# A transformer block on one core: instruction order from another timing model, pair sums split once, and two late loads in a chain of their own

## The chip, the cores and the metric

The kernel runs on one core of a Trainium2 chip. The metric is the device time of one execution in microseconds (us). The core has five engines that take instructions from queues of their own, each in order: TensorE (PE, with its weight loads listed apart as PEld), VectorE (DVE), ScalarE (ACT), GpSimd (POOL) and SyncE (SP), whose queue issues nearly all loads here.

## The reference, cut to what matters

One block over 512 tokens of width 1024, in float32. Eight heads use dilated attention ("a" heads), eight use compressed, selected and window attention with gates ("b" heads). A vector `c` gives shifts, scales and gate rows.

```python
mod = silu(c) @ w_ada + b_ada
sh1, sc1, g1, sh2, sc2, g2 = split(mod, 6)
u = layer_norm(x) * (1 + sc1) + sh1
o_a = dilated_attention(rope(qa), rope(ka), va)
o_b = nsa_attention(rope(qb), kc, vc, ks, vs, kw, vw, gates, ...)
y = concat([o_a, o_b]) @ w_o
x = layer_norm(ALPHA * x + g1 * y, ln1_g, ln1_b)
u = layer_norm(x) * (1 + sc2) + sh2
a_gate, a_val = split(u @ w_up, 2)
h = gelu(causal_dwconv(a_gate, conv_w, conv_b)) * a_val
x = layer_norm(ALPHA * x + g2 * (h @ w_down), ln2_g, ln2_b)
```

## The kernel before, in words

Every matrix operand is a pair: a value rounded to the matmul type (`hi`) and the rest (`lo`). `split` (L255) makes the two: ACT copies to `hi`, DVE or POOL subtracts. `mm3` (L259) then makes three matmuls, hi·hi, hi·lo, lo·hi (lines L260 to L262).

The stages are these. From 0 to about 66 us: layer norm of `x`, its transposes, the scale and shift columns of `c` (L351, on DVE), and the first product. From 66 to about 334 us: the attention rows, with the other input products ("quads", L1141 to L1148) as filler between them. From 334 to 380 us: the product with `w_o`, the residual norm and the second `u`. From 380 to 734 us: the up product (22 column blocks) and the down product (22 row blocks). At the end: the last norm and the output.

**The attention loop** (L1304 to L1320) has an iteration counter k over 76 rows and 5 more iterations. In each iteration the letters of `SEQ` say what is emitted: scores, weights, exponent, transposes and use of rows at fixed distances, filler matmuls (`f`), and four times `m`, which advances one background chain by one step (`run_misc`, L1084). A chain is a generator; `yield n` means that its next step comes no sooner than n calls of `run_misc` later. A row is emitted for scores at iteration k and its weighted sum ("use") five iterations later.

**The late chain.** `AUX = ['kvg3']` (L117) makes one chain (`late_steps`, L1057), started before the loop: first the compressed keys (`k`: four weight loads, then matmuls L1163), then the compressed values (`v`, the same), then the gate row g1 (`g`: `ada_row`, L1036, with eight loads of 512 KB and eight DVE sums, L1020 and L1022, a bias row L1043 and two pairs of matmuls L1048), then the shift vector of the second norm (`3`: eight loads `ada_col`, eight DVE reductions L1031). All these loads, those of the quads (`w_quad`, L1117) and of `w_o` use the four buffers `wraw` (`NR = 4`), and all are issued in order by SP.

**Sums of the heads.** The weighted sum of a head pair lies in one PSUM bank (`pv`, one buffer), in two halves of 64 partitions for e = 0 and e = 1. `folded` (L791) copies one half with ACT (L796) into a `wk` buffer (three of them) and hands it on. For a dilated pair `fold_a` (L827) does the following for e = 0 and again for e = 1, each time on 64 partitions: DVE adds (L829), DVE rounds to `oh` (L834), POOL subtracts to `ol` (L838). For a "b" pair `fold_b` (L800) adds into `ysum`, `cmp_end` (L886) adds the compressed part, and `pair_split` (L846) rounds with DVE (L848) and subtracts with POOL (L852), on 128 partitions.

**Order.** Within `tile.TileContext` the framework does not keep the order in which the code is written: it keeps dependences, and orders each engine's instructions by a simulated execution in which an instruction is dispatched when its inputs are ready. On the chip this order is fixed: an instruction whose input is late holds up all behind it on its engine.

Of the kernel before, what the change touches and what calls it, by code (L numbers as in the profile page):

```python
# [11 lines left out]
F32R = mybir.dt.float32r  # L12
PSUM = bass.MemoryType.PSUM
ALU = mybir.AluOpType
AF = mybir.ActivationFunctionType
# [91 lines left out]
def body(ctx, tc, nc, a, out, dbg=None):  # L107
    dbg = dbg or {}
    FILL = (2, 2, 3, 4)
    GAP = 4  # L110
# [3 lines left out]
    HG = 12  # L114
    WG = 4
    WK = 70
    AUX = ['kvg3']  # L117
    CP = 0
    YBS = (2, 3)
    OWK = ()  # L120
    FA = 1
# [21 lines left out]
    FS = 1  # L143
    QS = 1
# [23 lines left out]
    V, A, P, T = nc.vector, nc.scalar, nc.gpsimd, nc.tensor  # L168
# [4 lines left out]
    def slot(tag, bufs, shape, dt=F32, name=None):  # L173
        return sb.tile(shape, dt, name=name or tag, tag=tag, bufs=bufs)
# [7 lines left out]
    def to(name, dt=F32R):  # L182
        return slot('o', NO, [128, 512], dt, name)

    def u8(name):
        return slot('u2', 4, [128, 4, 512], F32R, name)
# [11 lines left out]
    def wraw(shape=(128, 1024)):  # L198
        return slot('wr', NR, list(shape), F32, 'wraw')
# [7 lines left out]
    def wk(name, dt=F32):  # L207
        return slot('wk', NW, [128, 512], dt, name)
# [7 lines left out]
    wlive = [0]  # L216

    def wk_wait(n):
        while wlive[0] + n > NW:
            yield 'wait'  # L220
        wlive[0] += n
# [15 lines left out]
    def f(x):  # L237
        return x.bitcast(F32)

    def load(dst, src, queue=nc.sync):  # L240
        queue.dma_start(dst, src)
# [13 lines left out]
    def split(raw, hi, lo, lo_engine=V):  # L255
        A.activation(hi, raw, AF.Copy)  # L256
        lo_engine.tensor_sub(lo, raw, f(hi))  # L257
# [61 lines left out]
    for t in range(NT):  # L319
# [7 lines left out]
        else:  # L327
            nb = offset_of(ag, P if NBP else V)
            cs = [slice(0, 1024)]
            if t == 3:  # L330
                cs = [slice(0, X3), slice(X3, 1024)]
                if XV:
                    c = cs.pop(0)
# [38 lines left out]
    for j in range(KD):  # L372
# [18 lines left out]
        for term in terms:  # L391
            for i in range(2):
                cs = slice(256 * i, 256 * i + 256)
                for t in range(NT):
                    tk = slice(128 * t, 128 * t + 128)
                    o_ = accs[i][t // 2][:, 256 * (t % 2):256 * (t % 2) + 256]
# [388 lines left out]
        return [row(tiles) for tiles in ((0, 1), (2,), (3,))]  # L785

    oh, ol = [None] * 8, [None] * 8
    ysum = [None] * 4
    done_o = set()

    def folded(pv, e):  # L791

        mn, ot = (0, 64) if e == 0 else (64, 0)
        yield from wk_wait(1)
        half = wk('fold')[mn:mn + 64]
        A.activation(half, pv[ot:ot + 64], AF.Copy)  # L796
        yield 2
        return half, pv[mn:mn + 64], slice(mn, mn + 64)
# [23 lines left out]
    def cmp_mm(h, pv, first):  # L822
        r = slice(64 * (h % 2), 64 * (h % 2) + 64)
        for i, (s_, p_) in enumerate(((0, 'h'), (1, 'h'), (0, 'l'))):
            T.matmul(pv, vpad[0][r, s_, :], pc[p_][h // 2][r], start=first and i == 0, stop=i == 2)

    def fold_a(idx, pv, e):  # L827
        half, own, mn = yield from folded(pv, e)
        V.tensor_add(half, own, half)  # L829
        if e == 0:  # L830
            mk = wk if idx in OWK else to
            oh[idx], ol[idx] = to('oh', F32R), mk('ol', F32R)
        yield 1
        (V.tensor_copy if FA else lambda o_, i_: A.activation(o_, i_, AF.Copy))(oh[idx][mn], half)  # L834
        yield 1
        for x in range(FS):
            c = slice(512 // FS * x, 512 // FS * (x + 1))
            P.tensor_sub(ol[idx][mn][:, c], half[:, c], f(oh[idx][mn][:, c]))  # L838
            if x < FS - 1:
                yield 1  # L840
        wlive[0] -= 1
        if e == 1:
            done_o.add(idx)
        yield 1

    def pair_split(h):  # L846
        oh[h], ol[h] = to('oh'), to('ol')
        V.tensor_copy(oh[h], ysum[h])  # L848
        yield 1
        for x in range(QS):  # L850
            c = slice(512 // QS * x, 512 // QS * (x + 1))
            P.tensor_sub(ol[h][:, c], ysum[h][:, c], f(oh[h][:, c]))  # L852
            if x < QS - 1:
                yield 1
        done_o.add(h)

    held = {}

# [166 lines left out]
    def ada_late_cols(gap, which=(2, 3)):  # L1025
        for i in which:
            for j in range(KD):
                w = wgem()
                load(w, a['ada_col'][j, i])
                yield gap  # L1030
                V.tensor_tensor_reduce(w, w, crow, 1.0, 0.0, op0=ALU.mult, op1=ALU.add, accum_out=mod[:, i, j:j + 1])  # L1031
            V.tensor_add(mod[:, i, :], mod[:, i, :], bcol[:, i, :])
            if i == 2:
                V.tensor_scalar_add(mod[:, 2, :], mod[:, 2, :], 1.0)

    def ada_row(s, out_, gap=None):  # L1036
        res = []
        yield from ada_sum(s, res, gap)
        acc = res[0]
        b1 = wgem()  # L1040
        load(b1[0:1, :], a['b_row'][s:s + 1, :])
        yield gap
        V.tensor_add(acc[0:1, :], acc[0:1, :], b1[0:1, :])  # L1043
        yield 2
        for h in range(2):
            yield from acc_wait()
            pr = acc_bank('gr')
            T.matmul(pr, ones, acc[:, 512 * h:512 * h + 512], start=True, stop=True)  # L1048
            yield 2
            A.activation(acc[:, 512 * h:512 * h + 512], pr, AF.Copy)  # L1050
            acc_done()
        out_.append(acc)
        yield

    g1l, g2l = [], []

    def late_steps(gap, AUX):  # L1057
        for c in AUX:
            if c == 'k':
                yield from hidden(kc_r, 'k_w1', P, comp_keys)  # L1060
            if c == 'v':
                yield from hidden(vc_t, 'v_w1', P, comp_values)
            if c == 'g':
                yield from ada_row(0, g1l, gap)
            if c == 'c':
                yield from ada_late_cols(gap)
            if c == '2':
                yield from ada_late_cols(gap, (2,))
            if c == '3':
                yield from ada_late_cols(gap, (3,))  # L1070
# [10 lines left out]
    def start_misc(gen, early=False):  # L1081
        misc.insert(0 if early else len(misc), [0, gen])
# [16 lines left out]
    def fill_one():  # L1099
        r = next(fill, fill)  # L1100
        if r is fill and WF and wo_started[0]:
            next(wo_fill, None)
        return r
# [47 lines left out]
    def hidden(src, w1, eng, post):  # L1151
        bl = []
        for d in blocks_of(src, eng, bl):
            yield d
        w = wgem((128, 4, 256))
        load(w, a[w1][0])
        yield HG
        yield from acc_wait()
        acc = acc_bank('hid')
        for q in range(4):  # L1160
            for l in range(4):
                l_ = 4 * q + l
                T.matmul(acc[0:62, 0:256], bl[l_ // 8][:, l_ % 8, :], w[:, l, :], start=l_ == 0, stop=l_ == 15)  # L1163
                if l % 2 and l < 3:
                    yield
            if q < 3:
                w = wgem((128, 4, 256))
                load(w, a[w1][q + 1])
                yield HG
        yield 1  # L1170
        hs = bs('hs', F32)
        A.activation(hs[0:62, 0:256], acc[0:62, 0:256], AF.Copy)
        acc_done()
        yield 3
        yield from acc_wait()
        acc = acc_bank('hT')
        for c_ in range(2):
            T.transpose(acc[:, 62 * c_:62 * c_ + 62], hs[0:62, 128 * c_:128 * c_ + 128], ident[0:62, 0:62])
        yield 2
        yield from post(acc)  # L1180
# [30 lines left out]
    def wo_prep():  # L1211
        for k in range(KD):
            w = wraw()
            load(w, a['w_o'][k])
            yield WG
            if k < 4:
                g = u8('wo')
                hl = [[g[:, 2 * i + h] for h in range(2)] for i in range(2)]
            else:
                mk = bs if k < 6 else t2  # L1220
                hl = [[mk('woh') for _ in range(2)], [mk('wol') for _ in range(2)]]
            for h in range(2):
                split(w[:, 512 * h:512 * h + 512], hl[0][h], hl[1][h], P if k in WP else V)
                yield
            wo.append(hl)
# [56 lines left out]
    def ahead(n):  # L1282
        for _ in range(n):
            fill_one()
# [10 lines left out]
    ahead(PRE)  # L1295
    for st_ in AUX:
        start_misc(late_steps(GAP, st_))
# [6 lines left out]
    for k in range(nrow + DT + DU):  # L1304
        n = FILL[rows[k]['n'] // 128 - 1] if k < nrow else 0
        if k >= WK and not wo_started[0] and ('a', 3) in ready:
            wo_started[0] = True
            start_misc(wo_prep())
        slots = SEQ.count('f')
        for op in SEQ:  # L1310
            if op == 'm':
                run_misc()
            elif op == 'f':
                for _ in range(n // slots):
                    fill_one()
                n, slots = n - n // slots, slots - 1
            else:
                name, d = steps_of[op]
                if 0 <= k - d < nrow:
                    rows[k - d][name]()  # L1320
# [151 lines left out]
    for fi in range(KF):  # L1472
        tg = tags[fi % 3]
        pg, pv = bank(tg[0], 'pg'), bank(tg[1], 'pvv')
# [62 lines left out]
    for t in range(NT):  # L1537
# [3 lines left out]
        for c0, c1 in zip(edges, edges[1:]):  # L1541
            h, cs = c0 // 512, slice(c0 % 512, (c1 - 1) % 512 + 1)
# [18 lines left out]
```

## Time and profile before

| | |
|---|---|
| median of 3 runs | 744.16 us (742.37 to 745.16) |
| the profiled execution's own time | 745.01 us |
| its span, first to last instruction | 742.8 us |
| instructions | 10888 |
| busy: PE, PEld, DVE, ACT, POOL | 94%, 81%, 64%, 45%, 42% |

The profiled execution lasts 2.2 us longer than its span, and 0.85 us longer than the median. Busy time is the union of an engine's instructions; ends of matmuls are modelled, so a PE that counts as busy may still have room.

### The profile page before, as it was taken

How to read it: one execution, taken by the hardware profiler on the slowest of the kernel's cores; microseconds unless marked ns; L12 is line 12 of the kernel's file. 1: busy time of each engine (PE TensorE's matmuls, PEld its weight loads, DVE VectorE, ACT ScalarE, POOL GpSimd, SP SyncE). 2: the span in 40 equal slices, each digit the busy share in tenths (PEclk: the TensorE clock that was granted, in tenths of full speed). 3: DMA queues.
4: the chain of work that ended last, by engine and by line, in shares of the span. 5: the costliest groups of instructions: out<-in, count | busy, mean ns of one | idle time of the engine just before them, and what ended most of it. 6: DMA issues, size and time to landing. Idle time of an engine off the chain costs nothing.

```text
span 742.8 us, 10888 instructions
## 1 busy us (share of the span) xinstructions
PE 696.2 (94%) x3964; PEld 598.1 (81%) x3964; DVE 476.2 (64%) x981; ACT 333.8 (45%) x677; POOL 310.7 (42%) x307
## 2 busy tenths in 40 slices
PE   8789799999999887989999999999999999999995
PEld 6779778988898876777898888888888888888884
DVE  6997975763699998989854334455553433444436
ACT  5235566664666476843654333333433432223101
POOL 3335573944478737461211111011011147666216
PEclk8999999999999999999999999999999999999998
DMA  9942632122444522063102323444332225334002
GB/s 321 386 172 90 227 136 75 47 86 86 143 133 151 172 86 86 1 224 116 54 5 85 108 91 115 141 142 150 133 126 102 85 86 156 127 120 137 28 15 99
DMA packets 29149, 89.93 MB, mean 121 GB/s; under 512 B 3748, under 2 KB 4516, under 8 KB 29096
## 3 DMA queue, kind: packets, MB, share of 16 engines
q1 hardware_dynamic: 28516, 89.05, 34.8%
q8 instruction: 31, 0.51, 0.3%
q10 hardware_dynamic: 580, 0.19, 0.1%
q14 instruction: 22, 0.18, 0.1%
HBM read 87.13 MB, written 2.10 MB: 120 GB/s over the span
## 4 chain that ended last, share of the span: by engine, by line
PE 49%; DVE 3%; POOL 1%; issue 0%; ACT 0%; POOLq 0%; DVEq 0%
PE d L261 5%; PE d L262 5%; PE d L260 5%; PE pvv L262 5%; PE pvv L260 5%; PE pvv L261 5%; PE pg L260 5%; PE pg L262 5%; PE pg L261 5%; DVE x L1370 1%; DVE bn L302 0%; PE wo L262 0%; DVE x L1361 0%; PE wo L260 0%; PE wo L261 0%
## 5 line engine op out<-in xcount | busy, mean ns | idle before, releaser
L257 DVE TENSOR_TENSOR wlo<-wraw,whi 128x1024 fp32r<-128x1024 f32 x60 | 80.8, 1347 | 123.4 <-ACT whi L256 122.2
L256 ACT ACTIVATE whi<-wraw 128x1024 fp32r<-128x1024 f32 (+1 forms) x68 | 70.5, 1036 | 149.3 <-PE pg L261 71.1
L260 PE MATMUL quad<-whi,u 128*128 128x256 f32 x256 | 76.7, 300 | 0.3 <-ACT gxz L523 0.3
L261 PE MATMUL quad<-wlo,u 128*128 128x256 f32 x256 | 73.1, 285 | 0.2 <-POOL wlo L1128 0.2
L262 PE MATMUL quad<-whi,u 128*128 128x256 f32 x256 | 72.6, 284 | 0.0
L257 POOL TENSOR_TENSOR hl<-cv,hh 128x512 fp32r<-128x512 f32 x14 | 22.3, 1596 | 119.7 <-ACT hh L256 119.7
L1513 POOL TENSOR_TENSOR wraw<-wraw,arow 128x1024 f32<-128x1024 f32 x22 | 60.4, 2763 | 25.5 <-DMA wraw<-w_down 25.5
L260 PE MATMUL pg<-u,whi 128*128 128x512 f32 (+1 forms) x176 | 67.7, 385 | 0.0
L261 PE MATMUL pg<-u,whi 128*128 128x512 f32 (+1 forms) x176 | 66.8, 380 | 0.0
L262 PE MATMUL pvv<-u,wlo 128*128 128x512 f32 (+1 forms) x176 | 66.8, 379 | 0.0
L262 PE MATMUL pg<-u,wlo 128*128 128x512 f32 (+1 forms) x176 | 66.8, 379 | 0.0
L261 PE MATMUL pvv<-u,whi 128*128 128x512 f32 (+1 forms) x176 | 66.8, 379 | 0.0
L260 PE MATMUL pvv<-u,whi 128*128 128x512 f32 (+1 forms) x176 | 66.8, 379 | 0.0
L1128 POOL TENSOR_TENSOR wlo<-wraw,whi 128x512 fp32r<-128x512 f32 x32 | 46.2, 1460 | 30.5 <-ACT whi L1125 30.5
L710 DVE CUSTOM_DVE_ANT_0 p<-sp,masks 128x128 f32<-128x128 f32 (+1 forms) x96 | 44.9, 481 | 14.7 <-PE sp L703 13.5
L260 PEld LDWEIGHTS quad<-whi,u 128*128 128x128 f32 x256 | 49.2, 192 | 5.7 <-issue 4.3
L261 PEld LDWEIGHTS quad<-wlo,u 128*128 128x128 f32 x256 | 49.3, 193 | 1.7 <-issue 0.5
L262 PEld LDWEIGHTS quad<-whi,u 128*128 128x128 f32 x256 | 49.0, 192 | 0.1
L257 POOL TENSOR_TENSOR hg<-cv,hg 128x512 fp32r<-128x512 f32 x8 | 12.9, 1612 | 75.1 <-ACT hg L256 75.1
L729 PE MATMUL pT<-ident,p 128*128 128x128 f32 x240 | 40.4, 283 | 4.2 <-POOL p L724 3.8
L260 PEld LDWEIGHTS pg<-u,whi 128*128 128x128 f32 x176 | 33.1, 188 | 6.6 <-issue 0.5
L261 PEld LDWEIGHTS pg<-u,whi 128*128 128x128 f32 x176 | 33.1, 188 | 6.6 <-issue 0.5
(637 smaller groups left out, 1928.5 us busy)
## 6 DMA issues: line engine op xcount, KB each, us to landing
wraw<-w_up SPq DMA_DIRECT2D x44, 512.0 KB, 3.3
wraw<-w_down SPq DMA_DIRECT2D x22, 512.0 KB, 3.3
ada<-ada_col SPq DMA_DIRECT2D x32, 256.0 KB, 6.1
wraw<-w_quad SPq DMA_DIRECT2D x16, 512.0 KB, 4.1
wraw<-ada_col SPq DMA_DIRECT2D x16, 512.0 KB, 3.7
wraw<-ada_row SPq DMA_DIRECT2D x16, 512.0 KB, 3.2
x<-x SPq DMA_DIRECT2D x8, 512.0 KB, 4.7
wraw<-w_o SPq DMA_DIRECT2D x8, 512.0 KB, 4.1
```

The costliest lines, as they stand in the source:

```text
L256: A.activation(hi, raw, AF.Copy)
L257: lo_engine.tensor_sub(lo, raw, f(hi))
L260: T.matmul(o_, sh, mh, start=start, stop=False)
L261: T.matmul(o_, sh, ml, start=False, stop=False)
L262: T.matmul(o_, sl, mh, start=False, stop=stop)
L710: V.tensor_tensor_reduce(p[:, cols[i]], e['s'][:, cols[i]], masks[:, m0:mask0 + 512], 1.0, 3e38, op0=ALU.add, op1=ALU.min, accum_out=m_[:, ...
L729: T.transpose(e['t'][:, 128 * j:128 * j + 128], e['p'][:, 128 * j:128 * j + 128], ident)
L1128: P.tensor_sub(wl[:, p:p + PS], w[:, p:p + PS], f(wh[:, p:p + PS]))
L1370: V.scalar_tensor_tensor(src[:, hs], src[:, hs], ag[:, 3:4], b_[h][:, cs], op0=ALU.mult, op1=ALU.add)
L1513: P.tensor_mul(w, w, g2)
```

## The change

It does five things. The framework's order is now made by its timeline simulator (`schedule_with_timeline_sim=True`) in place of its default simulator: this holds for every instruction of the kernel. The late chain before the loop is cut to `kv`; `g` and `3` form a second chain, started at iteration k = 22. `fold_a` for e = 0 only copies and adds into its half of a `ysum` buffer, which is a `wk` buffer kept until e = 1 is done; after e = 1 one rounding and one subtraction on 128 partitions follow, through `pair_split`. `pair_split` rounds with ACT in place of DVE, for both kinds of pair. `ysum` has eight places.

```diff
-    AUX = ['kvg3']
+    AUX = ['kv']
...
+    def pair_split(h):
+
+        oh[h], ol[h] = to('oh'), to('ol')
+        A.activation(oh[h], ysum[h], AF.Copy)
+        yield 1
+        P.tensor_sub(ol[h], ysum[h], f(oh[h]))
+        done_o.add(h)
+
     def fold_a(idx, pv, e):
-        half, own, mn = yield from folded(pv, e)
-        V.tensor_add(half, own, half)
+
+        mn, ot = (0, 64) if e == 0 else (64, 0)
         if e == 0:
-            mk = wk if idx in OWK else to
-            oh[idx], ol[idx] = to('oh', F32R), mk('ol', F32R)
+            yield from wk_wait(1)
+            ysum[idx] = wk('fold')
+        half = ysum[idx][mn:mn + 64]
+        A.activation(half, pv[ot:ot + 64], AF.Copy)
+        yield 2
+        V.tensor_add(half, pv[mn:mn + 64], half)
         yield 1
-        (V.tensor_copy if FA else lambda o_, i_: A.activation(o_, i_, AF.Copy))(oh[idx][mn], half)
-        yield 1
-        for x in range(FS):
-            c = slice(512 // FS * x, 512 // FS * (x + 1))
-            P.tensor_sub(ol[idx][mn][:, c], half[:, c], f(oh[idx][mn][:, c]))
...
         if e == 1:
-            done_o.add(idx)
-        yield 1
-
-    def pair_split(h):
-        oh[h], ol[h] = to('oh'), to('ol')
-        V.tensor_copy(oh[h], ysum[h])
...
+            yield from pair_split(idx)
+            wlive[0] -= 1
+            yield 1
...
             start_misc(wo_prep())
+        if k == 22:
+            start_misc(late_steps(GAP, 'g3'))
...
-    with tile.TileContext(nc) as tc:
+    with tile.TileContext(nc, schedule_with_timeline_sim=True) as tc:
```

## Rows read from the trace of the kernel before

**Rows 1.** Stretch, length; busy us (instructions) of PE, PEld, DVE, ACT, POOL; clock, DMA.

```profile
0.00:66.00 66.00, 55.08 (x371) 49.47 (x372) 57.72 (x134) 22.93 (x34) 23.77 (x26) 0.95 0.72 256
66.00:150.00 84.00, 77.61 (x576) 69.47 (x576) 61.62 (x186) 53.72 (x136) 55.44 (x69) 1.00 0.35 122
150.00:200.00 50.00, 47.35 (x343) 41.06 (x341) 25.00 (x64) 28.14 (x67) 24.31 (x37) 1.00 0.30 103
200.00:250.00 50.00, 45.42 (x341) 42.97 (x341) 47.05 (x120) 30.73 (x79) 36.77 (x31) 0.97 0.46 154
250.00:334.00 84.00, 72.17 (x481) 62.46 (x482) 77.25 (x208) 57.04 (x149) 49.48 (x63) 0.98 0.30 102
...
380.00:734.00 354.00, 354.00 (x1619) 294.88 (x1619) 162.21 (x175) 116.02 (x152) 105.59 (x58) 1.00 0.31 105
```

**Rows 2.** The longest waits of PE, 200 to 334 us: total us, times, longest.

```profile
PE qT L464 <- POOL yq L429: 3.8, 1, 3.8
PE pT L729 <- POOL p L724: 2.8, 2, 2.0
PE sp L702 <- DVE pc L648: 1.7, 1, 1.7
PE pvb L777 <- DVE y L805: 1.7, 1, 1.7
PE pvb L777 <- DVE fold L829: 1.5, 1, 1.5
PE vcp L615 <- DVE gd L608: 1.2, 1, 1.2
PE pcT L667 <- DVE pc L648: 1.1, 1, 1.1
PE wo L262 <- POOL ol L838: 0.7, 1, 0.7
```

**Rows 3.** Groups of instructions, 200 to 334 us: count | busy us, mean ns | idle before.

```profile
L834 DVE CAST oh<-fold 64x512 fp32r<-64x512 f32 x8 | 3.6, 451 | 0.1
L848 DVE CAST oh<-y 128x512 fp32r<-128x512 f32 x4 | 2.0, 504 | 0.0
L838 POOL TENSOR_TENSOR ol<-fold,oh 64x512 fp32r<-64x512 f32 x8 | 14.5, 1809 | 9.2 <-DVE oh L834 9.2
L852 POOL TENSOR_TENSOR ol<-y,oh 128x512 fp32r<-128x512 f32 x4 | 5.1, 1282 | 3.4 <-DVE oh L848 3.4
L1125 ACT ACTIVATE whi<-wraw 128x512 fp32r<-128x512 f32 x8 | 4.8, 633 | 0.0
```

**Rows 4.** The same view: the DVE work of the gate row.

```profile
L1022 DVE SCALAR_TENSOR_TENSOR arow<-wraw,ccol,arow 128x1024 f32<-128x1024 f32 x6 | 9.7, 1618 | 0.0
L1043 DVE TENSOR_TENSOR arow<-arow,wraw 1x1024 f32<-1x1024 f32 x1 | 1.2, 1211 | 0.0
```

**Rows 5.** Timeline, start us and us: a fold, loads issued, ACT, DVE's first sum.

```profile
153.66 0.59 ACT L796 ACTIVATE fold<-pvb 64x512 f32<-64x512 f32 x1
...
176.42 5.00 SPq L241 DMA_DIRECT2D wraw<-w_quad  x2
...
182.74 1.15 ACT L1125 ACTIVATE whi<-wraw 128x512 fp32r<-128x512 f32 x2 [5.59 <-PE quad L262]
...
186.00 0.33 SPq L241 DMA_DIRECT2D wraw<-ada_row  x1
...
189.26 0.75 DVE L1020 TENSOR_SCALAR arow<-wraw,ccol 128x1024 f32<-128x1024 f32 x1 [10.69 <-DMA wraw<-ada_row]
```

**Rows 6.** SP's own waits, 140 to 260 us, then landing times of that window.

```profile
SPq L241 <- POOL wlo L1128: 67.8, 9, 15.5
...
wraw<-w_quad SPq DMA_DIRECT2D x6, 512.0 KB, 4.1
```

**Rows 7.** One line's instructions, whole run: ns min/median/max.

```profile
L353 DVE SCALAR_TENSOR_TENSOR mod<-part,b_col x16: 205/218/1851, 13.6 to 59.2; 128x1 f32<-128x1 f32 x16
L1022 DVE SCALAR_TENSOR_TENSOR arow<-wraw,ccol,arow x14: 1257/1285/2049, 198.0 to 536.9; 128x1024 f32<-128x1024 f32 x14
```

More of the change, by code (lines that the diff above doesn't have):

```diff
@@ L787, in body @@
     oh, ol = [None] * 8, [None] * 8
-    ysum = [None] * 4
+    ysum = [None] * 8
     done_o = set()
@@ L825, in cmp_mm, with fold_a @@
             T.matmul(pv, vpad[0][r, s_, :], pc[p_][h // 2][r], start=first and i == 0, stop=i == 2)
-    def fold_a(idx, pv, e):
-        half, own, mn = yield from folded(pv, e)
-        V.tensor_add(half, own, half)
-        if e == 0:
-            mk = wk if idx in OWK else to
-            oh[idx], ol[idx] = to('oh', F32R), mk('ol', F32R)
-        yield 1
-        (V.tensor_copy if FA else lambda o_, i_: A.activation(o_, i_, AF.Copy))(oh[idx][mn], half)
-        yield 1
-        for x in range(FS):
-            c = slice(512 // FS * x, 512 // FS * (x + 1))
-            P.tensor_sub(ol[idx][mn][:, c], half[:, c], f(oh[idx][mn][:, c]))
[L839 to L842, printed above, removed]
-            done_o.add(idx)
-        yield 1
     def pair_split(h):
         oh[h], ol[h] = to('oh'), to('ol')
-        V.tensor_copy(oh[h], ysum[h])
+        A.activation(oh[h], ysum[h], AF.Copy)
         yield 1
[L850 to L854, printed above, removed]
-        done_o.add(h)
+        P.tensor_sub(ol[h], ysum[h], f(oh[h]))
+        done_o.add(h)
+    def fold_a(idx, pv, e):
+        mn, ot = (0, 64) if e == 0 else (64, 0)
+        if e == 0:
+            yield from wk_wait(1)
[5 more added lines that the diff above has]
+        yield 1
+        if e == 1:
+            yield from pair_split(idx)
+            wlive[0] -= 1
+            yield 1
     held = {}
```

## The prediction

> **What bounds the kernel.** I read the table of busy time by stretch first [rows 1]. From 380 to 734 us PE is busy for 354 of 354 us: the up and down products are bound by matmuls there, and another order of the same matmuls gives nothing back. After it only a short norm chain runs, which the change leaves as it is. So what can be gained is PE's idle time before. By the same rows it is 66 − 55.08 = 10.9 us up to 66, 84 − 77.61 = 6.4 up to 150, 50 − 47.35 = 2.7 up to 200, and (50 − 45.42) + (84 − 72.17) = 16.4 from 200 to 334: 36.4 us in all, with the opening warm-up and first loads inside it.
>
> The stretch with most of it, 200 to 334 us, is also the one in which DVE is nearly full: 47.05 + 77.25 = 124.3 of 134 us, against 25.0 of 50 us just before, from 150 to 200. ACT has 134 − 30.73 − 57.04 = 46.2 us to spare there, POOL 47.8. The list of PE's waits says who ends them [rows 2]: of its eight longest entries the DVE ones come to 1.7 + 1.7 + 1.5 + 1.2 + 1.1 = 7.2 us and the POOL ones to 3.8 + 2.8 + 0.7 = 7.3. So from 200 to 334 PE and DVE share the bound, with POOL behind DVE.
>
> **The change, part by part.**
>
> *Pair sums.* Removed from DVE: 8 roundings at 451 ns and 4 at 504 ns, 3.6 + 2.0 = 5.6 us [rows 3]. Added to ACT: 8 roundings of 128x512; the nearest row is ACT's own rounding of that shape, 633 ns, so 8 x 0.633 = 5.1 us, hidden in ACT's 46.2 idle us (without that cover it would be 5.1). POOL: 8 subtractions of 1809 ns (14.5 us) become 4 of the 128-partition shape, 4 x 1.282 = 5.1 us: 9.4 us less [rows 3]. The copies and additions stay. What is a microsecond taken from DVE worth? Between nothing (PE is the bound) and PE's waits on DVE over the DVE time that leaves in this and the next part: 7.2 / (5.6 + 10.9) = 0.44. I take 0.3, nearer to the upper end because DVE is so full: 5.6 x 0.3 = **1.7 us**, bounds 0 to 5.6 x 0.44 = 2.4. For POOL the bounds are 0 and its 7.3 us of PE waits; most of those are at lines that the change doesn't touch (L429, L724), so I take 0.1 of 9.4, **0.9 us**. A row of its own speaks against the move: ACT's 633 ns is 0.18 us longer than DVE's 451, and the last pair's rounding stands right before the last subtraction that PE waits for (0.7 us) [rows 2, 3], so up to 0.2 us is lost once. [...]
>
> *A wait added.* The `wk` buffer of a dilated pair is now held from e = 0 to the end of e = 1. Behind it, in ACT's queue, stands the evacuation of a quad into `wk`, and behind that POOL's rotation, for which PE waited 3.8 us once [rows 2]. A post holds two of the three buffers and the sum one, so they fit; I cost it at nothing and keep 3.8 us as its upper end.
>
> *The second chain.* `g` and `3` start at k = 22. The third fold is emitted in that iteration and runs at 153.66 us; the first load of the gate row goes out at 186.0 us before [rows 5], so the chain moves forward by some 32 us. One chain step needs four calls of `run_misc`, one iteration. Ten steps of `g` then end near the time at which the eight sums now begin, and `3` takes their place. So 6 of the sums and the bias row, 9.7 + 1.2 = 10.9 us of DVE, leave the stretch after 200 us; the eight reductions of `3` only move inside it [rows 4]. Those 10.9 us land in 150 to 200, where DVE has 25.0 idle us [rows 1]; without that cover they would cost their 10.9. Worth 10.9 x 0.3 = **3.3 us**, bounds 0 to 10.9 x 0.44 = 4.8. The chain also moves its 17 loads, past two or three loads each of the compressed values and the quads in SP's queue and the four `wraw` buffers; that is the second rival. Two pairs of matmuls move with it and cost PE the same in either place.
>
> *The order.* The trace doesn't show what another model would order. Gain at most: PE's idle time before 200, 36.4 − 16.4 = 20.0 us [rows 1]. Loss: five more waits like PE's longest, 3.8 + 2.0 + 1.7 + 1.7 + 1.5 = 10.7 us [rows 2]. The nearest row is an error of the present order: DVE stood 10.69 us before the first sum, its load being late [rows 5]; but no PE wait of size lies in that stretch (2.7 us of idle in all [rows 1]). So removing such an error is worth little, and I take **1.1 us**.
>
> *Sum:* 1.7 + 0.9 + 3.3 + 1.1 = 7.0 us. The profiled execution (745.01, of which 742.8 is span) is 0.85 above the median of 744.16; less 7.0 it would give 738.0, and on the median **737.2 us**.
>
> **The rivals.**
>
> *DVE and POOL get in each other's way, and all the idle time comes back.* A one-column DVE instruction, 205 ns at its shortest, took 1851 ns, and the 1257 ns sum took 2049 [rows 7]. If this is the other engine's instruction being waited out, each microsecond taken from POOL also returns one to DVE: 5.6 + 10.9 + 9.4 = 25.9 us of 124.3, more than PE's 16.4 idle us of that stretch, so all 16.4 would go, and with 1.1 for the order it is 744.2 − 17.5 = **726.7 us**. [...] Against it: PE's matmuls in the stretch still count as busy 117.6 of 134 us, and chains of score, exponent and transpose stay.
>
> *The loads get in each other's way (slower).* Place: SP's queue from 150 to 190 us. Four `wraw` buffers serve values, quads and now the gate row; SP waited up to 15.5 us for one buffer [rows 6], and in order, so a gate load that waits holds a quad load behind it. Of the two quad loads from 176.42 the first lands some 4.1 us later, at 180.5 [rows 5, 6]; ACT takes it at 182.74, having waited for a matmul and not for the load [rows 5]. The lead is 2.2 us: from there on a delay is paid by the filler matmuls. A delay of the longest kind costs 15.5 − 2.2 = 13.3 us, so 737.2 + 13.3 = **750.5 us**. For it: a chain more in the same buffers. Against it: DMA is at a share of 0.30 there [rows 1], and the steps are spaced.
>
> *Nothing measurable.* The new order is nearly the old one, and the DVE time that leaves was hidden behind PE: about **744 us**. For it: PE counts as busy for 117.6 of 134 us even in the stretch at issue. Against it: DVE is busy for 92.8% of it, exactly where its work is taken away [rows 1].
>
> **How the numbers follow.** Half a percent, 3.7 us, is about what a measurement of this kernel can tell from no change. The forecast case, 731 to 740.4 with the likeliest value 737.2, gets 0.38; the first rival, below 731, 0.22; nothing measurable, 740.4 to 747.9, 0.20; the load rival and any other loss by the new order, above 747.9, 0.20. So faster 0.60, same 0.20, slower 0.20. The range reaches from 724 (the first rival with 2.7 us more from the order) to 751 (the second rival's price); it leaves out some 0.08 below and 0.11 above. The forecast case's own range is 731 to 740.4.
>
> **What would show it.** In the profile after: no DVE rounding of a head sum, 8 ACT ones near 0.63 us, 8 POOL subtractions of 128 partitions near 1.28; the first gate-row load well before 186 us and no later quad load; DVE below 45 us of busy time in the 50 us after 200, and PE's idle time from 200 us to the end of attention at 10 us or less; the up and down stretch at 354 us, only earlier. It is wrong if the idle time before 66 us or the dense stretch changes by more than 3 us (then the order is the story), if PE waits for quad weights, or if DVE's time falls and PE's idle time doesn't.

## The result and the profile after

The changed kernel takes **756.31 us** (median of 4 runs, 755.29 to 757.11) where the kernel before took 744.61 in the same series: a ratio of 1.0166, 95% interval 1.0147 to 1.0184. It is slower by some 12 us; 737.2 was forecast, and 756.31 lies above the range. The profiled execution took 755.98 us, with a span of 754.1 us.

Busy time by stretch of the kernel after, to be read against [rows 1]; columns as there, the last but two being the granted clock.

```profile
0.00:66.00 66.00, 56.93 (x401) 52.41 (x402) 54.53 (x133) 24.28 (x35) 27.45 (x28) 0.97 0.73 260
66.00:150.00 84.00, 74.27 (x514) 65.86 (x513) 58.23 (x179) 48.67 (x124) 45.12 (x58) 0.92 0.34 117
150.00:200.00 50.00, 46.15 (x337) 40.31 (x335) 34.07 (x68) 27.23 (x67) 31.77 (x42) 1.00 0.49 173
200.00:250.00 50.00, 46.31 (x341) 44.01 (x342) 41.14 (x120) 32.80 (x86) 24.79 (x34) 0.90 0.38 134
250.00:334.00 84.00, 78.75 (x523) 68.88 (x523) 69.48 (x197) 63.08 (x160) 42.04 (x61) 0.96 0.22 76
334.00:400.00 66.00, 56.80 (x310) 49.32 (x309) 43.20 (x101) 27.86 (x79) 13.00 (x19) 0.90 0.14 48
...
392.00:746.00 354.00, 353.48 (x1588) 294.20 (x1588) 162.34 (x175) 115.52 (x151) 106.84 (x58) 0.99 0.31 105
```

The same view of the kernel before, from 334 to 400 us.

```profile
334.00:400.00 66.00, 64.00 (x389) 56.84 (x388) 49.66 (x107) 35.59 (x87) 13.40 (x20) 1.00 0.19 67
```

Three things are to be seen. *The last stretch* is again PE nearly from end to end, 353.48 of 354 us; a few us of it run at a lower clock, which the last section shows. *By 334 us* PE has done 401 + 514 + 337 + 341 + 523 = 2116 instructions, against 371 + 576 + 343 + 341 + 481 = 2112 before, so it is not behind in number; but from 334 to 400 it does 310 against 389, with 66 − 56.80 = 9.2 us idle against 2.0. *The clock* is below 1.00 in five of the six stretches up to 400 us. The trace shows two levels: in pieces of 0.5 us, 93 of the 1506 pieces of the span stand at 0.50, 1396 at 1.00 and 17 in between (before: 31, 1444 and 9 of 1484). So twice the missing share times the length is the time at the lower level: 4.0 + 13.4 + 10.0 + 6.7 + 13.2 = 47 us up to 400; before it was 6.6 + 3.0 + 3.4 = 13 us [rows 1]. Over the whole span PE is busy 705.2 us for the 3964 instructions that took 696.2 before: of the 11.3 us by which the span grew, 9.0 are more busy time for the same instructions, 2.3 are more idle time. More busy time goes into the same matmuls at a lower clock (27 in 5.00 busy us at 0.55 and 44 at 1.00, in the last section), and also where they follow one another less closely (of the entries of 0.28 us there, one adds 0.12 us where the next starts 0.12 us behind it, and all of its 0.28 before a wait); the table doesn't tell the two apart.

The waits on POOL that were to go did go. PE's longest waits from 200 to 334 us, against [rows 2]: the longest by POOL is now 0.2 us.

```profile
PE pva L777 <- DVE fold L844: 2.5, 1, 2.5
PE pT L729 <- DVE pTl L752: 2.3, 2, 1.7
PE pvc L825 <- DVE pcl L677: 1.1, 1, 1.1
PE quad L260 <- DVE qo L473: 1.0, 1, 1.0
```

The end of the rows is to be seen in their last weighted sums: count, ns min/median/max, first and last start in us. First the kernel before, then the kernel after.

```profile
L777 PE MATMUL pva<-pTl,va x32: 274/282/283, 198.2 to 326.1; 128*128 128x256 f32 x24, 128*128 128x128 f32 x8
L777 PE MATMUL pva<-pTl,va x32: 274/282/561, 195.5 to 342.9; 128*128 128x256 f32 x24, 128*128 128x128 f32 x8
```

The last one begins 16.8 us later. What follows it, up to the end of the span, is no longer than before: 754.1 − 342.9 = 411.2 us for 742.8 − 326.1 = 416.7. So the kernel is slower because its rows end later.

The instructions of the roundings (ACT, L830) and subtractions (POOL, L832), whole run: count, ns min/median/max. They are the forecast 8 near 0.63 us and 8 near 1.28 us, against [rows 3].

```profile
L830 ACT ACTIVATE oh<-fold x4: 619/626/632, 215.8 to 344.6; 128x512 fp32r<-128x512 f32 x4
L830 ACT ACTIVATE oh<-y x4: 621/626/632, 283.7 to 316.7; 128x512 fp32r<-128x512 f32 x4
...
L832 POOL TENSOR_TENSOR ol<-fold,oh x4: 1286/1290/1297, 216.5 to 345.3; 128x512 fp32r<-128x512 f32 x4
L832 POOL TENSOR_TENSOR ol<-y,oh x4: 1282/1290/1297, 284.4 to 317.7; 128x512 fp32r<-128x512 f32 x4
```

### The profile page after: what moved, and what is told of

It is laid out like the page before. It is cut to its first block, busy times and chain, and to the rows that moved or that the text cites. A ratio compares the mean times of both kernels' runs of the same rounds, so it can differ in the third digit from the quotient of the medians.

```text
span 754.1 us, 10905 instructions
## 1 busy us (share of the span) xinstructions
PE 705.2 (94%) x3964; PEld 607.5 (81%) x3964; DVE 465.2 (62%) x969; ACT 336.7 (45%) x685; POOL 295.0 (39%) x303
## 4 chain that ended last, share of the span: by engine, by line
PE 73%; DMA 9%; DVE 7%; issue 4%; ACT 3%; POOL 3%; SPq 0%; POOLq 0%; DVEq 0%; ACTq 0%
PE pg L261 5%; PE pg L260 5%; PE pg L262 5%; PE pvv L261 5%; PE d L261 5%; PE d L262 5%; PE d L260 5%; PE pvv L262 5%; PE pvv L260 5%; DMA wraw<-ada_col 3%; PE pT L729 3%; PE quad L260 3%; PE quad L262 3%; PE quad L261 2%; DMA wraw<-ada_row 2%
## 5 line engine op out<-in xcount | busy, mean ns | idle before, releaser
L260 PE MATMUL quad<-whi,u 128*128 128x256 f32 x256 | 76.7, 300 | 2.8 <-ACT p L716 1.8
L261 PE MATMUL quad<-wlo,u 128*128 128x256 f32 x256 | 74.9, 293 | 0.0
L262 PE MATMUL quad<-whi,u 128*128 128x256 f32 x256 | 74.5, 291 | 0.0
L710 DVE CUSTOM_DVE_ANT_0 p<-sp,masks 128x128 f32<-128x128 f32 (+1 forms) x96 | 44.4, 486 | 18.8 <-PE pT L729 13.2
L260 PEld LDWEIGHTS quad<-whi,u 128*128 128x128 f32 x256 | 50.6, 198 | 5.8 <-issue 3.1
L1122 POOL TENSOR_TENSOR wlo<-wraw,whi 128x512 fp32r<-128x512 f32 x32 | 42.4, 1345 | 21.7 <-ACT whi L1119 21.7
L262 PEld LDWEIGHTS quad<-whi,u 128*128 128x128 f32 x256 | 50.6, 198 | 0.4
```

The costliest lines, as they stand in the source:

```text
L260: T.matmul(o_, sh, mh, start=start, stop=False)
L261: T.matmul(o_, sh, ml, start=False, stop=False)
L262: T.matmul(o_, sl, mh, start=False, stop=stop)
L710: V.tensor_tensor_reduce(p[:, cols[i]], e['s'][:, cols[i]], masks[:, m0:mask0 + 512], 1.0, 3e38, op0=ALU.add, op1=ALU.min, accum_out=m_[:, ...
L1122: P.tensor_sub(wl[:, p:p + PS], w[:, p:p + PS], f(wh[:, p:p + PS]))
```

## The experiments

Ratios are to the kernel before in the same series, with 95% intervals. "Old order" is that of the default model, "new order" that of the timeline model. The letters in the expectations: O, the new order costs by itself; C, the second chain collides; F, the pair sums; H, DVE's waits for loads of columns in the opening; G, PE's filler stands ahead of the rows; D, the orders of DVE, ACT and POOL put waiting instructions at the heads of queues.

**The parts one by one.** First the flag alone, put on the kernel before:

```diff
-    with tile.TileContext(nc) as tc:
+    with tile.TileContext(nc, schedule_with_timeline_sim=True) as tc:
```

> The kernel before with the new order alone. Theory O (the new order is what costs): it is as slow as the changed kernel or slower, 753 to 765 us, with at least 25 us of TensorE clock at half before the up product. Theory C (the chain started at k = 22 collides with other loads and sums): it stays at 744 us, within 3. Theory F (the pair sums, rounded late and on ACT, delay the end of attention): 744 us as well.

Measured: 765.09 us, 1.0286 (1.0252 to 1.0320). Then the changed kernel without the flag, so both edits in the old order:

```diff
-    with tile.TileContext(nc, schedule_with_timeline_sim=True) as tc:
+    with tile.TileContext(nc) as tc:
```

> The changed kernel with the old order: pair sums and second chain only. Theory O: the two edits are worth what was forecast for them or a part of it, 737 to 743 us, and the half-clock time stays near that of before (14 us before the end). Theories C and F: 750 us or more, since the edit at fault is still in it.

Measured: 740.17 us, 0.9964 (0.9943 to 0.9984). So the order is the whole loss, and the edits without it are a gain. Next, each edit taken out of the changed kernel. With the one chain:

```diff
-    AUX = ['kv']
+    AUX = ['kvg3']
...
-        if k == 22:
-            start_misc(late_steps(GAP, 'g3'))
```

> The changed kernel with the gate row and the shift vector back in the first chain; new order, new pair sums. Theory O: still slow, 752 us or more. Theory C: the loss goes, 745 us or less. Theory F: 755 us, as the changed kernel.

Measured: 765.47 us, 1.0314 (1.0252 to 1.0376). With the old pair sums:

```diff
-            ysum[idx] = wk('fold')
...
+        half, own, mn = yield from folded(pv, e)
+        V.tensor_add(half, own, half)
...
-        A.activation(oh[h], ysum[h], AF.Copy)
+        V.tensor_copy(oh[h], ysum[h])
```

> The changed kernel with the pair sums of before; new order, second chain. Theory O: still slow, 755 to 762 us (the edit's gain of some 2 us missing). Theory C: 756 us. Theory F: the loss goes, 746 us or less.

Measured: 756.42 us, 1.0162 (1.0139 to 1.0184). In the new order the chain is worth 9 us and the pair sums nothing. In the old order it is the other way round. The chain alone, on the kernel before:

```diff
-    AUX = ['kvg3']
+    AUX = ['kv']
...
+        if k == 22:
+            start_misc(late_steps(GAP, 'g3'))
```

> The kernel before with the second chain alone, old order. If the chain carries what the two edits gain together in the old order (3 us): 740 to 741 us. If the forecast's sizes hold (3.3 us for the chain, 2.6 for the sums): 741 us. If its loads collide as in the second rival: 744 us or more.

Measured: 745.45 us, 1.0018 (1.0000 to 1.0036). DVE's waits from 60 to 345 us and the stretch 150 to 200 of this kernel:

```profile
DVE arow L1022 <- DMA wraw<-ada_row: 9.6, 6, 3.4
...
DVE arow L1020 <- DMA wraw<-ada_row: 3.0, 1, 3.0
```

```profile
150.00:200.00 50.00, 45.16 (x316) 38.27 (x317) 33.38 (x66) 25.46 (x58) 26.49 (x35) 1.00 0.48 171
```

DVE waits 9.6 + 3.0 = 12.6 us for the gate row's loads, no less than the 10.69 before [rows 5], only in seven pieces; and PE's busy time in that stretch falls from 47.35 to 45.16 us. The waits moved; they did not go. The quad loads go out later as well: the fifth of the ten from 100 us on at 167.56 us for 159.84, the eighth at 210.12 for 187.81, and PE does 159 quad matmuls from 150 to 200 us for 189. But no engine is seen to wait for a quad load. The pair sums alone, on the kernel before:

```diff
-    ysum = [None] * 4
+    ysum = [None] * 8
...
-        V.tensor_copy(oh[h], ysum[h])
+        A.activation(oh[h], ysum[h], AF.Copy)
...
+            ysum[idx] = wk('fold')
```

> The kernel before with the new pair sums alone, old order. Forecast's size: 1.7 + 0.9 = 2.6 us, 741 us. If DVE's and POOL's time there was hidden behind PE: 743 us, no difference.

Measured: **739.50 us, 0.9939 (0.9919 to 0.9959)**, faster than the kernel before and the changed kernel. Its stretches from 200 us:

```profile
200.00:250.00 50.00, 45.12 (x340) 42.67 (x340) 45.51 (x118) 32.05 (x82) 32.35 (x31) 0.97 0.46 157
250.00:334.00 84.00, 75.10 (x502) 64.77 (x503) 76.81 (x207) 61.85 (x155) 43.06 (x62) 1.00 0.34 117
```

From 250 to 334 PE does 502 instructions where it did 481 [rows 1], with 8.9 us idle for 11.8, and the clock is whole.

**Candidates inside the new order.** In the new order DVE stands early on before the column loads of an early chain, `2` (`ada_col`; 6.7 us once in the changed kernel). This moves that chain behind the keys and values of the late one, in the changed kernel and in its old-order twin:

```diff
-    AUX = ['kv']
+    AUX = ['kv', '2']
...
-    EAUX = ['2']
+    EAUX = []
```

> The changed kernel (new order) with the scale column's eight loads and DVE reductions moved from the opening of the attention stage to a chain started with the loop. Theory H (in the new order DVE reductions stand at the head of the queue before their load has landed, 12 us of DVE waiting, and the first rows start 8 us late): half or more of the loss goes, 750 us or less, and the first transposes of rows start before 98 us. Theory G (the order puts filler ahead of rows everywhere, PE then has gaps and its clock falls): 753 to 757 us, with half-clock time above 35 us still.

> The same move in the old order, with both edits. From 66 to 100 us DVE is busy 31 of 34 us and the eight reductions are 10 us of it, so the first rows may start earlier: 736 to 740 us if rows at the opening are bound by DVE, 740 to 743 if PE is.

Measured: 756.91 us, 1.0156 (1.0130 to 1.0181) in the new order; 745.57, 1.0013 (0.9994 to 1.0033) in the old. The transposes of the weights (`pT`) in the changed kernel and, moved, in this one, a line of each:

```profile
L729 PE MATMUL pT<-ident,p x240: 270/272/474, 103.3 to 336.7; 128*128 128x128 f32 x120
```

```profile
L729 PE MATMUL pT<-ident,p x240: 270/272/476, 93.8 to 337.3; 128*128 128x128 f32 x120
```

The first row starts 9.5 us sooner and the last begins where it did: an early delay is not what sets the end, and theory H falls. In the old order the move costs some 0.5% (1.0013 for 0.9964), which neither reading expected. The next two take the `w_o` product, which PE begins among the last rows, and write it after the rows: the changed kernel, and the pair sums alone.

```diff
-    WF = 1
+    WF = 0
```

> The changed kernel, new order, with the early product with w_o written after all rows and not between them (the order may still pull it forward). Theory G: if its place in the text decides, 746 to 752 us and weighted sums that end before 338 us; if readiness in the model decides, 756 us, no change. Theory D: 756 us.

> Control: new pair sums, old order, and the same early product written after all rows. In the old order rows are slower with less filler between them only if TensorE had gaps to fill: 739 to 744 us under both theories.

Measured: 753.91, 1.0137 (1.0111 to 1.0163), and 741.18, 0.9951 (0.9931 to 0.9971): no measurable difference from their parents. In the new order the model pulled the product forward all the same, its first matmul at 288.7 us for 289.9, so this kernel tells nothing of a later `w_o`. Two more tie PE's work behind the rows: each `w_o` matmul, then each quad matmul too, is issued after the last row instruction written before it.

```diff
+    def behind():
+        return tc.issue_after(last_row[0]) if last_row[0] is not None else nullcontext()
...
-                mm3(wo_acc[h], oh[k][:, 0:128], ol[k][:, 0:128], wo[k][0][h], wo[k][1][h], k == 0, k == KD - 1)
+                with behind():
+                    mm3(wo_acc[h], oh[k][:, 0:128], ol[k][:, 0:128], wo[k][0][h], wo[k][1][h], k == 0, k == KD - 1)
```

> The changed kernel, new order, with one tie: each early matmul of the product with w_o is queued on TensorE behind the attention row instruction written before it. Theory G (the new order puts filler ahead of rows in TensorE's queue; the product with w_o is used up before the last rows end, so the norm chain after it has no cover, TensorE idles and its clock falls): fewer than 70 of the 196 early matmuls by the end of the weighted sums in place of 106, weighted sums ending before 338 us in place of 343, 746 to 752 us. Theory D (the new order on DVE, ACT and POOL is what costs, with heads of queues that wait): 754 us or more.

> The same tie for the input products' filler matmuls as well. Theory G: TensorE's order is then close to the written one between rows and filler, the first transposes of rows start before 100 us, half-clock time below 30 us, 738 to 748 us. Theory D: 752 us or more, since only TensorE's order is tied.

Measured: 757.93, 1.0180 (1.0155 to 1.0204), and 767.42, 1.0311 (1.0292 to 1.0331). In the first of them `w_o` begins 23.6 us later than the 289.9 us of the changed kernel and yet the last weighted sums (`pva`) begin only 1 us sooner there:

```profile
L268 PE MATMUL wo<-wo,oh x32: 387/392/517, 313.5 to 364.0; 128*128 128x512 f32 x32
```

```profile
L785 PE MATMUL pva<-pTh,va x32: 222/282/522, 195.5 to 341.8; 128*128 128x256 f32 x24, 128*128 128x128 f32 x8
```

The tie was weaker than meant: 82 `w_o` matmuls still stand before the end of the rows, for 99 in the changed kernel, where fewer than 70 were expected. Holding the quads back too makes the kernel 11 us slower than the changed one, where theory G had it faster. So the rows do not simply wait for PE to be free of filler; theory G falls, and PE's old order, taken whole below, says the same.

**Which stage, and which engine.** For the rest I fixed orders outright: the instructions of an engine were chained, by edges of the class `NoSync`, meant to set the order of issue and no wait, in the order that they have in one of the two kernels (the changed one, or its old-order twin). Three kernels with all five engines fixed take the new order up to a point and the old one behind it.

```diff
+            traced = list(nc.cur_bb.bb.instructions)
+            for text in ORDERS.values():
...
+                for p_, q_ in zip(at, at[1:]):
+                    tc.add_manual_dep(traced[q_], traced[p_].name, mybir.DependencyInfo(mybir.DependencyClass.NoSync, mybir.DependencyReason.DATA), reason='order')
```

> Both edits; every engine's order is fixed: the first 395 of PE's 3898 instructions, and what the timeline model placed before the last of them on any engine, stand in the new order (the stage up to some 66 us), all the rest in the old one. With the whole old order this kernel took 740.2, with the whole new one 756.3: the question is in which stage the 16 us lie. Theory Opening (the new order loses its 8 us of the opening for good): 748, half of the loss here. Theory Rows (the loss is made between the attention rows): 740 to 742. Theory Norm (made after the last weighted sum): 740 to 742.

> The same with the cut at PE's 1240th instruction (some 200 us). Theory Opening: 748. Theory Rows: 747 to 750, about half of the 16 us, as a share of the rows is in the new order. Theory Norm: 740 to 742.

> The same with the cut at PE's 2100th instruction (some 334 us; the last weighted sums), so that only the residual norm, its transposes and what follows stand in the old order. Theory Opening: 748. Theory Rows: 754 to 757, all of the loss. Theory Norm: 740 to 743, the loss is gone.

| new order up to | us | ratio |
|---|---|---|
| nowhere (both edits, old order) | 740.17 | 0.9964 (0.9943 to 0.9984) |
| 66 us | 738.29 | 0.9917 (0.9888 to 0.9947) |
| 200 us | 744.09 | 0.9989 (0.9973 to 1.0005) |
| 334 us | 755.04 | 1.0148 (1.0119 to 1.0177) |
| the end (the changed kernel) | 756.31 | 1.0166 (1.0147 to 1.0184) |

The loss is made between the rows: 1.0148 − 0.9917 = 2.3%, or 17 us, of which 0.7% by the part of the order up to 200 us and 1.6% by the part from 200 to 334. The opening costs nothing, and neither does the norm behind the rows. (The kernel cut at 200 us lies in none of the three ranges given for it: slower than theory Norm had it, faster than the other two.) The stretches 200 to 334 and 334 to 400 of the kernels cut at 200 and at 334 us:

```profile
200.00:334.00 134.00, 122.51 (x859) 109.91 (x859) 113.00 (x319) 96.30 (x245) 66.33 (x95) 0.96 0.28 97
334.00:400.00 66.00, 64.52 (x390) 57.14 (x389) 47.98 (x106) 33.50 (x85) 13.50 (x20) 1.00 0.16 57
```

```profile
200.00:334.00 134.00, 125.66 (x876) 114.77 (x874) 110.50 (x316) 94.42 (x241) 64.62 (x91) 0.94 0.28 97
334.00:400.00 66.00, 52.16 (x308) 45.27 (x307) 44.68 (x103) 29.94 (x82) 13.23 (x19) 0.92 0.11 40
```

With the new order from 200 to 334 PE is busier there, 125.66 for 122.51 us, and does 876 instructions for 859: by its busy time the stretch looks better. But the rows end later. Their last weighted sums, of the kernel cut at 200 and then of that cut at 334:

```profile
L777 PE MATMUL pva<-pTl,va x32: 273/282/561, 194.2 to 328.0; 128*128 128x256 f32 x24, 128*128 128x128 f32 x8
L777 PE MATMUL pva<-pTl,va x32: 275/282/561, 195.0 to 340.1; 128*128 128x256 f32 x24, 128*128 128x128 f32 x8
```

What PE does more of is `w_o`; the quads are 288 matmuls in both. PE's `w_o` matmuls in the same stretch, in the same two kernels (busy us, count, clock, DMA):

```profile
200.00:334.00 134.00, 13.95 (x50) 0.96 0.28 97
200.00:334.00 134.00, 20.26 (x79) 0.94 0.28 97
```

The last weighted sum begins 12.1 us later, which is all of the loss: what follows it takes 752.8 − 340.1 = 412.7 us of the span for 742.5 − 328.0 = 414.5. The `w_o` work done early gives back no more than these 1.8 us, since PE then has 66 − 52.16 = 13.8 us with nothing to do from 334 on, most of it in waits for the norm chain (12.8 us for ACT's `xh`), although the order there is the old one again. What the other engines waited for in those rows is in ACT's waits from 200 to 345 us, of the kernel cut at 200 and then of that cut at 334:

```profile
ACT pTh L748 <- PE pT L729: 5.1, 6, 1.6
...
ACT fold L842 <- PE pva L777: 2.4, 4, 1.2
```

```profile
ACT pTh L748 <- PE pT L729: 15.3, 14, 3.1
ACT fold L842 <- PE pva L777: 7.2, 5, 5.6
```

ACT stands 22.5 us before transposes and weighted sums that PE has not come to, against 7.5. That goes along with the later end; it doesn't show its cause. Is it then PE's order? Three kernels give some engines the order of one model and let the other model order the rest around it: PE's old order inside the timeline model; DVE, ACT and POOL in their old order with PE by the timeline model; and DVE, ACT and POOL in their new order with PE by the default model. The edges are those above, on the engines named; SP's queue of loads is left to the model in all three. Theory M, in the last two, was set down when the first had been measured.

> Both edits and the timeline model, but PE's 3898 instructions are fixed in the order of the old model; the other engines are ordered by the timeline model around that. Theory P (PE's own order, where rows and filler and w_o stand, costs): 740 to 743. Theory D (the orders of DVE, ACT and POOL cost, whose heads of queue wait): 752 to 757.

> Both edits and the timeline model, but DVE, ACT and POOL are fixed in the order of the old model; PE is ordered by the timeline model around that (its order differs from the old one in about as many pairs as the new one does). Theory D (the orders of DVE, ACT and POOL make the loss, PE's follows): 740 to 745. Theory P (PE's own order makes it): 752 to 757. Theory M (no single engine: what counts is that all were made together, and a mixture is as bad or worse): 757 or more.

> The counterpart: both edits and the default model, but DVE, ACT and POOL are fixed in the order of the timeline model; PE is ordered by the default model around that. Theory D: 752 to 757, the loss stays. Theory P: 740 to 745, the loss goes. Theory M: 757 or more.

Measured: 763.20, 1.0246 (1.0223 to 1.0269); 768.96, 1.0345 (1.0328 to 1.0362); 779.93, 1.0481 (1.0459 to 1.0503). All three are slower than the changed kernel. Theory P falls by the first (PE in its old order, `w_o` begun at 313.4 us, and yet the last weighted sum at 347.0), theory D by the second. No engine's order can be named as the bad one. Theory M agrees with all three, but that an order is good only with the orders that it was made with isn't shown by them alone: where some engines are fixed, the others get an order that neither kernel had. The rows from 200 us of the last of them:

```profile
200.00:334.00 134.00, 118.85 (x775) 105.62 (x775) 99.78 (x283) 85.24 (x217) 61.06 (x89) 0.88 0.27 92
334.00:400.00 66.00, 59.62 (x298) 48.85 (x298) 43.25 (x100) 28.88 (x73) 16.97 (x25) 0.94 0.20 68
```

PE does 775 instructions from 200 to 334 where the changed kernel does 341 + 523 = 864, and the clock is 0.88.

## Why the prediction was wrong

**The order: the step that failed.** It was taken as a gain of 1.1 us, with a loss of at most 10.7 as the other end. Alone it costs 0.0286 x 744.16 = 21 us (19 to 24), and on top of the edits some 15 (1.0166 − 0.9964 = 2.0%), which leaves the changed kernel 12 us slower. Two things in the step were wrong. The loss was priced as five more waits like PE's longest: but PE's idle time from 200 to 334 us fell, from 16.4 to 8.9 us, and grew by 2.3 us over the whole span. What the runs show in its place is a later end of the rows, 342.9 us for 326.1, with other engines waiting for PE (22.5 us of ACT's in the kernel cut at 334 us for 7.5 in that cut at 200). And an order was treated as something that is corrected at one place, the sum that stood 10.69 us before its load [rows 5]; the flag reorders every engine's queue, and the mixtures show that this cannot be priced by one queue.

**The pair sums** had the right sign, and the term was too small: 1.7 + 0.9 = 2.6 us forecast, 0.0061 x 744.16 = 4.5 us measured (3.1 to 6.0) in the old order. The wait added on `wk` was costed at nothing, which agrees. In the new order the same edit is worth nothing (756.42 without it, 756.31 with it). No run tells its DVE part from its POOL part. The 0.18 us that it was said to lose once compared two shapes; on 128x512 DVE takes 504 ns [rows 3], and the difference is 0.13.

**The second chain** was to bring 3.3 us and brings none in the old order (745.45 us, 0.0 to 2.7 us of loss). DVE's work on the gate row (`arow`) did leave the stretch 200 to 334 us as forecast, 11.88 us before, 1.10 with the chain alone and none in the changed kernel; what was left out is that its sums stand at the head of DVE's queue before loads that come no faster there (12.6 us of DVE's waits in the chain alone for 10.69 before). In the second rival's place there is the later quad load that it speaks of, but no wait for one, and the interval of the chain alone reaches down to no loss: that its mechanism cost anything isn't shown. In the new order it is worth 9 us by the medians (765.47 without it, 756.31 with it): one cannot add these terms across orders.

**The signs named** came out as said for the roundings, the subtractions and DVE's 45 us. The first gate-row load goes out at 161.88 us, 24 us sooner where some 32 were forecast, but quad loads are later, the fifth from 100 us on at 170.45 us for 159.84 and the eighth at 206.84 for 187.81. The dense stretch keeps its length and comes later, not earlier. PE's idle time from 200 to 334 us is 3.69 + 5.25 = 8.9 us, and no more up to 343 us, under the 10 that were named as a sign of success, and the kernel is 12 us slower. The two signs that were to show the order as the story did not appear either: the idle time before 66 us is 9.1 for 10.9, and the last stretch is 353.48 for 354. Idle time was the wrong measure: it counts neither which instructions PE does nor how long each takes. The rival "nothing measurable" fell, as the interval of the changed kernel begins at 1.0147; the first rival fell too: of the 16.4 idle us of that stretch 8.9 are left, and the time did not follow. Whether DVE and POOL hold each other up, as it has it, no run tested.

**What stays open.** Why the timeline model's order is the worse one, whether by its durations or by its landing times of loads, was not tried, and what in the new order makes the rows end later is open: neither `w_o` nor PE's order alone accounts for it. Nor was the clock taken apart from the order, as no run held it up in the new order. The time at the lower level isn't simply the loss: up to 400 us it is 13 us before, some 35 in the kernel cut at 200 us, which takes no longer than the kernel before, and some 45 in that cut at 334. That the kernel cut at 66 us beats the pair sums alone isn't shown: the intervals overlap.

## What to carry to other kernels

Take a scheduler's flag as a change of its own, time it alone first, and keep it out of the sum of other edits: here it cost 21 us and hid a gain of 0.6% that one edit had by itself. Judge an order by when the last due work ends, here the last weighted sum, and not by how busy the engine is: 125.66 busy us of 134 were worse than 122.51. Giving some engines one order and the rest another is no repair: all three such kernels were slower than with either order alone.

## What was not expected of the hardware

Behind two waits PE's instructions took longer with no further wait: 0.41 us and more for 0.28. The end of the norm chain in the changed kernel: the two waits for ACT, and the 128x256 matmuls behind them (start us, us).

```profile
387.82 0.28 PE L261 MATMUL pvv<-u,upw 128*128 128x256 f32 x1
387.94 0.28 PE L262 MATMUL pvv<-u,upw 128*128 128x256 f32 x1
390.07 1.35 PE L1399 MATMUL x1T<-ident,xh 128*128 128x128 f32 x8 [1.85 <-ACT xh L1390]
392.52 0.58 PE L260 MATMUL pg<-u,whi 128*128 128x256 f32 x1 [1.09 <-ACT u L1407]
392.90 0.42 PE L260 MATMUL pvv<-u,whi 128*128 128x256 f32 x1
393.11 0.41 PE L260 MATMUL pg<-u,upw 128*128 128x256 f32 x1
```

The same kernel in two stretches of 5 us behind that; columns as in [rows 1].

```profile
394.00:399.00 5.00, 5.00 (x27) 5.00 (x27) 1.33 (x7) 1.25 (x7) 0.00 (x0) 0.55 0.00 0
399.00:404.00 5.00, 5.00 (x44) 5.00 (x43) 2.03 (x3) 2.79 (x3) 0.00 (x0) 1.00 0.00 0
```

The same shape starts every 0.12 us before the pause (clock 1.00 from 385 to 388 us) and every 0.21 us behind it; PE is busy 5.00 of 5 us in both stretches and does 27 instructions at a granted clock of 0.55 (0.50 from 394 to 398 us) and 44 at 1.00. So more time went here than the two waits of 1.85 and 1.09 us and the eight short transposes between them (1.35 us), and the surplus is entered as busy time; that the waits brought the lower clock is what their order in time suggests, and no run tested it. What all of it cost isn't measured: PE's busy time grew by 9.0 us over the span, for whatever reason. Part of the time at the lower level PE is idle: from 200.6 to 210.8 us of the changed kernel the clock is 0.50, and PE is busy for 7.48 of 10.20 us.
